# One decoder step, first stage and attention: a PE order table, one transpose and the sample tables moved

## The chip, the core and the metric

The kernel runs on one core of one Trainium2 chip, in fp32. Its time is the device time of one execution in microseconds. The engines are named as the profile names them: PE (TensorE), ACT (ScalarE), DVE (VectorE), POOL (GpSimd), SP (SyncE).

## What is computed

One inference step of a one-layer decoder, for 512 prompt tokens and for 8 sequences of 8 sample tokens with 2048 cached tokens each. Forgetting attention (FoX) and sparse attention (NSA) run side by side on the same normed input:

```python
def layer_sample(x, c, fox_pool, logf_pool, nsa_pool, win_buf, page_table, lp):
    pm = pre_mixer(x, c, lp)          # h = rms_norm(x) * (1 + scale(c)) + shift(c); z = h @ w_in; split
    o_fox = fox_attend(...)           # over all cached keys, with forget gates
    nsa_all = jnp.concatenate([gather_pages(nsa_pool, page_table), pm['nsa_rows']], axis=1)
    kc, vc, c_end = compressed_kv(nsa_all[:, :, 0], nsa_all[:, :, 1], lp)
    o_nsa = nsa_attend(...)           # compressed, selected and window keys, three gates
    y = post_mixer(x, pm, o_fox, o_nsa, lp)   # branches, gates, output projection, MLP

def compress_blocks(x, pos, w1, w2):
    xc = x[:, :n_chunk * CMP_STRIDE].reshape(b, n_chunk, CMP_STRIDE, NSA_GROUPS, HEAD_DIM)
    lead = jnp.einsum('bncgd,cdh->bngh', xc + pos[0], w1[0])
    trail = jnp.einsum('bncgd,cdh->bngh', xc + pos[1], w1[1])
    return jnp.einsum('bngh,hd->bngd', jax.nn.silu(lead[:, :-1] + trail[:, 1:]), w2)
```

`compressed_kv` applies `compress_blocks` to the raw keys and values and norms the keys' result. The prompt's layer is the same without a cache.

## The kernel before

`Step.first_stage` (L549) compresses the cached keys and values. It works in 48 units: four pieces (j) by keys and values (kv) for batches 0, 1, 2 and 3 alone (units 0 to 31), then for batches 4 and 5 together (32 to 39) and 6 and 7 together (40 to 47). In a unit u:

- `cmp_order` (L458, asked two units ahead) copies a piece of the pages `cpg` into a tile `ro` on DVE (three buffers),
- `rows_turn` (L467), for unit u + 1, transposes `ro` on PE ("ct"), ACT copies the result to `x`, and the sum of its halves goes to `xs`: on DVE for one batch, on POOL (L485) for two,
- `cmp_hidden` (L487), for unit u, multiplies `x` and `xs` with the weights ("hid", "hids"),
- then the functions of `todo[u]` run, a table written out by hand (L614 to 664).

PE's order is the order of the calls: `link` (L93) chains each matmul and transpose behind the one before. The other engines' orders come from a scheduler that sees the dependences. From `todo` come, among others:

- for each of five x tiles `norm` (ACT square, DVE inverse root in small steps), `scaled` (ACT) and `turned` (eight PE transposes "nt", two ACT copies "adw<-nt"); the tuple (n, v, u) gives the three units, (28, 30, 31) and (29, 31, 33) for the last two,
- the eight parts of the modulation, `ada_first` ("ada" on PE, "adap" on ACT) and one unit later `ada_end` ("adat" on PE, a sum on DVE); `modulate` (L816) applies a pair of them to the turned tiles,
- `cmp_act` and `cmp_silu` (the activation of a group of units, "cst" and "csx"), `cmp_out` (products "co", keys then normed into "knn") at units 18/19, 34/35, 42/43, and `cmp_keys` (L542: two transposes "kct" of knn, one ACT copy) at units 21, 37, 45.

In this stage the PSUM tag "mm" has two banks, in turn for ada, nt's first half, nt's second half, adat, co and kct. A tile there waits until the reader of the tile two before has finished.

`prompt_attention` (L1083) runs in steps: four heads each of the selected ("slc"), window ("win") and FoX branches. A step asks the scores of its own head (`scores`, group 0), then the values of the head before last (`weigh`, L1343), then its scores of group 1, and the transposes of the head before (`turn_over`, `factors`). For a "slc" head, `cmp_turn` (L1388) transposes the compressed weights "cm" (four PE transposes "ct<-identF,cm" and a copy to the upper part of cm), called right behind `factors` (L1157); `weigh` uses the result in the "oc" products behind the sixteen "oslc" products.

`sample_tables` (L1554) is asked at step n = 9, so that it runs among the FoX heads. It makes masks and ramps for the sample attention: large ones on POOL (`gp`), 29 small ones on DVE (`self.ts`, `self.tt`, `self.cp`). POOL also makes the copies "ffox<-denfox" (`scale`, L1308) that PE's "fcfox" transposes (`factors`) read.

Of the kernel before, what the change touches and what calls it, by code (L numbers as in the profile page):

```python
# [11 lines left out]
OP = mybir.AluOpType  # L12
# [34 lines left out]
class Step:  # L47
# [501 lines left out]
    def first_stage(self, pl, pe, hf, seam):  # L549
# [69 lines left out]
        for k, (n, v, u) in enumerate(((18, 21, 23), (20, 23, 25), (22, 25, 27), (28, 30, 31), (29, 31, 33))):  # L619
            todo[n] += [lambda k=k: norm(k)]  # L620
            todo[v] += [lambda k=k: scaled(k)]
            todo[u] += [lambda k=k: turned(k)]
# [23 lines left out]
        for k, u in enumerate((26, 30, 32, 34, 36, 38, 40, 42)):  # L646
            todo[u] += [lambda k=k: ends.update({k: self.ada_first(pe, ada[k])})]
            todo[u + 1] += [lambda k=k: ends[k]()]
            if k > 1:
                todo[(27, 31, 33, 35, 37, 39)[k - 2]] += [wada(k)]  # L650
            if k % 2:
                todo[max(u + 2, 35)] += [lambda k=k: self.modulate(0, hf, range(k - 1, k + 1))]
# [8 lines left out]
        for i in range(3):  # L661
            for kv in range(2):
                todo[(18, 34, 42)[i] + 1 - kv] += [lambda i=i, kv=kv: self.cmp_out(pl, i, kv)]
            todo[(21, 37, 45)[i]] += [lambda i=i: self.cmp_keys(i)]
# [418 lines left out]
    def prompt_attention(self, pk, pn, pp):  # L1083
# [22 lines left out]
        for n, (br, r) in enumerate(steps + [(None, None)] * 2):  # L1106
# [49 lines left out]
            if prev:  # L1156
                held = pbr, pr, T, pf, self.cmp_turn(pr, pw) if pbr == "slc" else None  # L1157
# [185 lines left out]
    def weigh(self, pn, br, r, T, F, cT):  # L1343

        u = f"{br}{r}"
        out = self.oT[:, r + (0 if br == "fox" else 4), 0:SEQ]
# [207 lines left out]
    def sample_tables(self):  # L1554
# [19 lines left out]
        self.ts(hot, ei, self.prow, None, OP.is_equal)  # L1574
# [10 lines left out]
        for g in range(2):  # L1585
            nbf = self.carve([NS, NB, 8])
            self.tt(nbf, self.nbf[:, g], tmask[:NS], OP.add)
            own = self.nbA[g].rearrange("p (i x) -> p i x", x=80)
            for o in range(2):
                self.cp(own[32 * o:32 * o + 32, :, 8 * o:8 * o + 8], nbf[32 * o:32 * o + 32, o::2])  # L1590
        own = self.nbW.rearrange("p (i x) -> p i x", x=80)
        for o in range(2):
            self.cp(own[64 * o:64 * o + 64, :, 8 * o:8 * o + 8], tramp[64 * o:64 * o + 64, 0:4])
# [12 lines left out]
        self.ts(pos, self.h_row, 4.0, -4.0, OP.is_ge, OP.mult)  # L1606
        self.tt(pos, pos, self.h_row, OP.add)
        self.ts(lim, pos, 0.0, 4.0, OP.is_equal, OP.mult)
        self.tt(lim, lim, pos, OP.add)
        self.ts(self.tok, ej, lim, None, OP.is_lt)  # L1610
        self.ts(self.hot.rearrange("p (h t) -> p h t", t=8), ej[:, :, None].to_broadcast([P, 8, 8]), self.t_row, None, OP.is_equal)

        self.ts(pos, self.g_row, 15.0, 1.0, OP.mult, OP.add)
        self.ts(lim, self.prow, 64.0, slope, OP.is_ge, OP.mult)
        for g in range(2):
            self.ts(low[:, g:g + 1], lim, pos, 0.0625 ** g, OP.mult, OP.mult)
        step, new = self.carve([P, 4]), self.carve([P, 2, 8])
        self.iota(step, [[512, 4]], base=-2048)
        for g in range(2):
            self.ts(self.base[:, :, g], step, low[:, g:g + 1], None, OP.mult)  # L1620
            self.iota(new[:, g], [[1, 8]], base=512)
            self.ts(new[:, g], new[:, g], low[:, g:g + 1], None, OP.mult)
            self.tt(new[:, g], new[:, g], tmask[:, 0], OP.add)
            own = self.nbA[g].rearrange("p (i x) -> p i x", x=80)
            for o in range(2):
                v = slice(64 + 32 * o, 96 + 32 * o)
                self.cp(own[v, :, 8 * o:8 * o + 8], new[v, g, None, :].to_broadcast([32, 4, 8]))
# [1109 lines left out]
```

## Time and profile before

| | |
|---|---|
| median of 3 runs | 1149.58 us (1149.41, 1149.58, 1157.79) |
| profiled execution | 1149.83 us, span 1148.2 us |
| mean granted PE clock | 0.997 |
| HBM | 217.64 MB read, 57.12 MB written |

The profile has one execution. Times in it are microseconds from the span's start. A row of a timeline gives the start, the length, engine, line of kernel.py, operation and tiles (out<-in), a count where rows were joined, and in brackets the idle time of the engine ahead of the row with what ended it. Matmuls are pipelined, so that a row's length overlaps the next row. In a table of groups the numbers behind the bar are busy microseconds, mean nanoseconds of one, and idle time ahead. The first stage takes about the first 165 us of the span, prompt attention lies between about 290 and 430.

### The profile page before, as it was taken

What the parts mean: (1) busy time and instruction counts of PE and PEld (TensorE: products, weight loads), DVE (VectorE), ACT (ScalarE), POOL (GpSimd) and SP (SyncE); (2) the same over time, 40 slices, a digit from 0 to 9 for tenths busy, and PEclk for the clock granted to TensorE, in tenths of its full rate; (3) what the DMA queues carried; (4) which work ended last, traced back from release to release, by engine and by line L of the source; (5) the groups of instructions that cost most, each with busy time, mean ns of one, the idle gap of its engine ahead of it and who ended that gap; (6) DMA issues with size and microseconds to landing.
All of it is one profiled execution on the core that took longest, in us unless ns stands there. A gap on an engine that the chain in (4) does not pass through costs nothing.

```text
span 1148.2 us, 25279 instructions
## 1 busy us (share of the span) xinstructions
PE 1120.8 (98%) x9530; PEld 971.6 (85%) x9530; DVE 768.8 (67%) x1841; ACT 576.6 (50%) x1101; POOL 306.5 (27%) x366
## 2 busy tenths in 40 slices
PE   8989999999999999999999999999999999999998
PEld 5987889999676666777899999789999998888887
DVE  3655576686788875666654446668776754798686
ACT  1455453354777775555432324356565655565420
POOL 5313320000321150001666573001655511110000
PEclk9999999999999999999999999999999999999999
DMA  9998445796586587999889986356444537977732
GB/s 237 250 265 227 144 125 195 242 335 210 194 273 201 185 287 251 295 314 337 226 260 290 327 274 221 103 161 211 135 150 154 184 113 254 319 261 255 249 105 83
DMA packets 188188, 255.52 MB, mean 223 GB/s; under 512 B 23161, under 2 KB 144706, under 8 KB 185890
## 3 DMA queue, kind: packets, MB, share of 16 engines
q1 hardware_dynamic: 148770, 173.03, 48.5%
q0 software_dynamic: 21296, 67.38, 17.8%
q10 hardware_dynamic: 18000, 13.50, 3.9%
q8 instruction: 75, 1.23, 0.4%
q14 instruction: 47, 0.39, 0.1%
HBM read 217.64 MB, written 57.12 MB: 239 GB/s over the span
## 4 chain that ended last, share of the span: by engine, by line
PE 82%; DVE 8%; DMA 4%; issue 3%; ACT 2%; SPq 1%; POOL 1%; POOLq 0%; ACTq 0%; DVEq 0%
PE dn L83 14%; PE mg L83 9%; PE z L83 8%; PE br L83 4%; PE wo L83 3%; PE hid L83 3%; PE up L83 3%; PE k L89 3%; DMA cpg<-in_cache_nsa_kv 2%; PE ss L83 2%; PE so L83 2%; PE dns L83 2%; PE ct L89 2%; PE ada L83 1%; PE hids L83 1%
## 5 line engine op out<-in xcount | busy, mean ns | idle before, releaser
L83 PE MATMUL z<-winh,h 128*128 128x264 f32 (+1 forms) x576 | 110.5, 286 | 0.1
L83 PEld LDWEIGHTS z<-winh,h 128*128 128x128 f32 x576 | 91.6, 190 | 1.6 <-issue 0.8
L83 PE MATMUL z<-winl,h 128*128 128x264 f32 (+1 forms) x320 | 88.1, 284 | 0.2 <-DVE winl L137 0.2
L83 PE MATMUL mg<-hH,wmh 128*128 128x288 f32 x240 | 70.5, 295 | 0.0
L83 PE MATMUL mg<-hH,wml 128*128 128x288 f32 x240 | 70.2, 294 | 0.0
L83 PE MATMUL mg<-hL,wmh 128*128 128x288 f32 x240 | 68.5, 296 | 0.0
L83 PE MATMUL hid<-x,w1raw 128*128 128x128 f32 (+1 forms) x384 | 66.8, 318 | 0.2 <-ACT x L118 0.2
L83 PEld LDWEIGHTS z<-winl,h 128*128 128x128 f32 x320 | 60.6, 190 | 0.4 <-DVE winl L137 0.4
L83 PEld LDWEIGHTS hid<-x,w1raw 128*128 128x128 f32 x384 | 56.1, 197 | 3.4 <-ACT x L118 0.5
L118 ACT ACTIVATE x<-ct 128x512 f32<-128x512 f32 x64 | 36.4, 594 | 42.9 <-PE ct L89 28.5
L137 DVE TENSOR_TENSOR wml<-wmr,wmh 128x1024 fp32r<-128x1024 f32 x14 | 22.5, 1604 | 42.7 <-ACT wmh L118 42.7
L83 PEld LDWEIGHTS mg<-hH,wmh 128*128 128x128 f32 x240 | 45.1, 188 | 0.1
L83 PEld LDWEIGHTS mg<-hH,wml 128*128 128x128 f32 x240 | 45.0, 188 | 0.0
L83 PEld LDWEIGHTS mg<-hL,wmh 128*128 128x128 f32 x240 | 44.3, 188 | 0.0
L137 DVE TENSOR_TENSOR wp<-sums,wp 128x1024 fp32r<-128x1024 f32 x26 | 36.8, 1424 | 10.5 <-ACT wp L118 10.0
L137 DVE TENSOR_TENSOR wp<-pu,wp 128x512 fp32r<-128x512 f32 (+1 forms) x26 | 31.7, 1224 | 17.6 <-ACT wp L118 17.6
L118 ACT ACTIVATE mgt<-mg 128x288 f32<-128x288 f32 x32 | 12.6, 407 | 52.7 <-PE mg L83 52.6
L118 ACT ACTIVATE u<-u 128x1152 f32<-128x1152 f32 x29 | 33.6, 1159 | 10.8 <-DVE u L106 10.0
L2097 POOL TENSOR_TENSOR td<-td,td 128x512 f32<-128x512 f32 x24 | 33.2, 1384 | 21.2 <-DMA td<-in_w_down 20.5
L2097 POOL TENSOR_TENSOR td<-td 128x512 f32<-128x512 f32 x24 | 33.9, 1414 | 15.8 <-DMA td<-in_w_down 15.6
L89 PE MATMUL ct<-identF,ro 128*128 128x128 f32 x256 | 36.6, 277 | 1.5 <-DVE ro L121 1.5
L83 PE MATMUL br<-oL,wbh 128*128 128x288 f32 x128 | 37.8, 295 | 0.0
(1176 smaller groups left out, 3581.5 us busy)
## 6 DMA issues: line engine op xcount, KB each, us to landing
adw<-in_w_ada SPq DMA_DIRECT2D x16, 1024.0 KB
foxD<-in_cache_fox_kv SPq DMA_DIRECT2D x128, 128.0 KB
rows<-in_cache_nsa_kv SPq DMA_DIRECT2D x128, 128.0 KB
rows<-foxD SPq DMA_DIRECT2D x26, 512.0 KB
pu<-in_w_up SPq DMA_DIRECT2D x26, 512.0 KB
wdr<-in_w_down SPq DMA_DIRECT2D x26, 512.0 KB
cpg<-in_cache_nsa_kv SPq DMA_DIRECT2D x96, 128.0 KB
td<-in_w_down POOLq DMA_DIRECT2D x24, 512.0 KB, 6.3
```

Of the source, the lines that this page charges most:

```text
L83: ins = self.nc.tensor.matmul(out, a, b, start=start, stop=stop, skip_group_check=True)
L89: ins = self.nc.tensor.transpose(out, in_, self.identF[:n, :n])
L118: return self.nc.scalar.activation(out, in_, f, **kw)
L137: self.splits.append((eng or self.nc.vector).tensor_tensor(l, x, h.bitcast(F32), op=OP.subtract).ins)
L2097: self.nc.gpsimd.tensor_tensor(out, x, y, op=OP.subtract)
```

## The change

Four things move; nothing is added or left out.

1. In `first_stage` the keys' transposes go from units (21, 37, 45) to (24, 39, 46).
2. There too the last two x tiles go from (28, 30, 31) and (29, 31, 33) to (30, 32, 33) and (33, 36, 37), and `modulate` for the first two pairs of parts to unit 38 and 39 at the earliest.
3. `cmp_turn` is called at the head of `weigh`, one step later, and no longer behind `factors`.
4. The 29 small instructions of `sample_tables` go to POOL.

```diff
--- before.py
+++ after.py
@@ -616,7 +616,7 @@
         todo[10] += [self.ada_turned, lambda: self.cmp_bias(pe, 0), lambda: self.cmp_bias(pe, 1)]
         todo[12] += [self.cmp_bias_end]
 
-        for k, (n, v, u) in enumerate(((18, 21, 23), (20, 23, 25), (22, 25, 27), (28, 30, 31), (29, 31, 33))):
+        for k, (n, v, u) in enumerate(((18, 21, 23), (20, 23, 25), (22, 25, 27), (30, 32, 33), (33, 36, 37))):
             todo[n] += [lambda k=k: norm(k)]
             todo[v] += [lambda k=k: scaled(k)]
             todo[u] += [lambda k=k: turned(k)]
@@ -649,7 +649,7 @@
             if k > 1:
                 todo[(27, 31, 33, 35, 37, 39)[k - 2]] += [wada(k)]
             if k % 2:
-                todo[max(u + 2, 35)] += [lambda k=k: self.modulate(0, hf, range(k - 1, k + 1))]
+                todo[max(u + 2, 37 + (k + 1) // 2)] += [lambda k=k: self.modulate(0, hf, range(k - 1, k + 1))]
         self.lfg = {}
         for y, u in enumerate((32, 35)):
             todo[u] += [pinned(lambda y=y: self.stage_logf(pe, y))]
@@ -661,7 +661,7 @@
         for i in range(3):
             for kv in range(2):
                 todo[(18, 34, 42)[i] + 1 - kv] += [lambda i=i, kv=kv: self.cmp_out(pl, i, kv)]
-            todo[(21, 37, 45)[i]] += [lambda i=i: self.cmp_keys(i)]
+            todo[(24, 39, 46)[i]] += [lambda i=i: self.cmp_keys(i)]
         self.cmp_warm(50)
         self.cmp_order(pl, 0)
         self.cmp_taps(0)
@@ -1154,7 +1154,7 @@
             if prev:
                 pf = self.factors(pn, f"{pbr}{pr}", pF)
             if prev:
-                held = pbr, pr, T, pf, self.cmp_turn(pr, pw) if pbr == "slc" else None
+                held = pbr, pr, T, pf, pw
             prev = None
             if br is None:
                 continue
@@ -1340,9 +1340,11 @@
         self.act(F, tb)
         return F
 
-    def weigh(self, pn, br, r, T, F, cT):
+    def weigh(self, pn, br, r, T, F, cw):
 
         u = f"{br}{r}"
+        if br == "slc":
+            cT = self.cmp_turn(r, cw)
         out = self.oT[:, r + (0 if br == "fox" else 4), 0:SEQ]
         ob = self.accb(f"o{u}")
         cv = {"slc": C_SV, "win": C_WV, "fox": C_FV}[br]
@@ -1571,7 +1573,7 @@
         ei, hot = self.carve([P, 32]), self.carve([P, 32])
         self.iota(ei, [[1, 32]])
-        self.ts(hot, ei, self.prow, None, OP.is_equal)
+        gp.tensor_scalar(hot, ei, self.prow, None, op0=OP.is_equal)
...
         for g in range(2):
             nbf = self.carve([NS, NB, 8])
-            self.tt(nbf, self.nbf[:, g], tmask[:NS], OP.add)
+            gp.tensor_tensor(nbf, self.nbf[:, g], tmask[:NS], op=OP.add)
             own = self.nbA[g].rearrange("p (i x) -> p i x", x=80)
             for o in range(2):
-                self.cp(own[32 * o:32 * o + 32, :, 8 * o:8 * o + 8], nbf[32 * o:32 * o + 32, o::2])
+                gp.tensor_copy(own[32 * o:32 * o + 32, :, 8 * o:8 * o + 8], nbf[32 * o:32 * o + 32, o::2])
...
-        self.ts(pos, self.h_row, 4.0, -4.0, OP.is_ge, OP.mult)
-        self.tt(pos, pos, self.h_row, OP.add)
...
+        gp.tensor_scalar(pos, self.h_row, 4.0, -4.0, op0=OP.is_ge, op1=OP.mult)
+        gp.tensor_tensor(pos, pos, self.h_row, op=OP.add)
...
```

PE in the first stage, units 20 to 24, before (hids and hid are the products of a unit, ct the turn of the next, kct the keys' transposes):

```order
L83 MATMUL hids_883<-xs_116,w1sum 128x128 x2
L89 MATMUL kct_1100<-identF,knn_973 128x128 x2
L89 MATMUL ct_1106<-identF,ro_3_996 128x128 x4
L83 MATMUL hid_881<-x_113,w1raw 128x128 x4
L83 MATMUL hids_883<-xs_114,w1sum 128x128 x2
```

and with the change:

```order
L83 MATMUL hids_883<-xs_116,w1sum 128x128 x2
L89 MATMUL ct_1102<-identF,ro_3_996 128x128 x4
L83 MATMUL hid_881<-x_113,w1raw 128x128 x4
L83 MATMUL hids_883<-xs_114,w1sum 128x128 x2
L89 MATMUL ct_1142<-identF,ro_0_1100 128x128 x4
L83 MATMUL hid_882<-x_115,w1raw 128x128 x4
L83 MATMUL hids_883<-xs_116,w1sum 128x128 x2
L89 MATMUL nt_00_1155<-identF,x_857 128x128 x4
L89 MATMUL nt_01_1161<-identF,x_857 128x128 x4
L89 MATMUL ct_1170<-identF,ro_0_1100 128x128 x4
L83 MATMUL hid_881<-x_113,w1raw 128x128 x4
L83 MATMUL hids_883<-xs_114,w1sum 128x128 x2
L89 MATMUL kct_1185<-identF,knn_973 128x128 x2
```

The kct transposes now stand behind three more units and the first x tile's nt.

ACT in the first stage around the copies of x tile 3's transposes (adw<-nt_30 and nt_31; nss is the sum of squares of a tile, nrs its inverse root), before:

```order
L118 ACTIVATE x_1187<-x_1187,nrs_3_1294 128x1024
L118 ACTIVATE cst_1474<-hid_882,cmpb 128x256
L118 ACTIVATE cst_1427<-csx_1426 128x512
L118 ACTIVATE x_1266<-x_1266,nrs_4_1379 64x1024
L118 ACTIVATE adw<-nt_30_1452 128x4x128
L118 ACTIVATE adw<-nt_31_1458 128x4x128
```

and with the change:

```order
L118 ACTIVATE cst_1439<-csx_1438 128x512
L118 ACTIVATE x_1183<-x_1183,nrs_3_1375 128x1024
L118 ACTIVATE adap_1478<-ada_1479 128x256
L118 ACTIVATE x_113<-ct_1493 128x4x128
L118 ACTIVATE x_113<-ct_1499 128x4x128
L118 ACTIVATE sq_1524,nss_4_1525<-x_1266 64x1024
L118 ACTIVATE adw<-nt_30_1512 128x4x128
L118 ACTIVATE adw<-nt_31_1518 128x4x128
```

The scaling of the last tile (x_1266, nrs_4) has left the place ahead of the adw copies, and its square (sq, nss_4) stands there.

POOL among the FoX heads, between the second and the third copy ffox, before (scr and fscr hold the tables):

```order
L1315 COPY ffox_5766<-denfox_5687 128x512
L1598 TENSOR_SCALAR scr<-scr,slope_i 128x512
L736 TENSOR_TENSOR fscr<-fscr,Dt 128x256
L1584 TENSOR_TENSOR scr<-scr 128x64
L1599 TENSOR_TENSOR scr<-scr 128x512
L738 TENSOR_TENSOR fscr<-fscr 128x8x8
L131 IOTA scr 128x512 x2
L739 TENSOR_TENSOR fscr<-fscr 128x8x8
L1630 TENSOR_SCALAR scr<-scr 128x512
L1315 COPY ffox_6025<-denfox_5948 128x512
```

and with the change:

```order
L1315 COPY ffox_5766<-denfox_5687 128x512
L1600 TENSOR_SCALAR scr<-scr,slope_i 128x512
L1610 TENSOR_SCALAR scr<-scr 128x1
L736 TENSOR_TENSOR fscr<-fscr,Dt 128x256
L1586 TENSOR_TENSOR scr<-scr 128x64
L1589 TENSOR_TENSOR scr<-nbf,scr 64x64 x2
L1601 TENSOR_TENSOR scr<-scr 128x512
L1611 TENSOR_TENSOR scr<-scr 128x1
L738 TENSOR_TENSOR fscr<-fscr 128x8x8
L1595 COPY scr<-scr 64x4x8 x2
L1592 COPY scr<-scr 32x4x8 x4
L1315 COPY ffox_6025<-denfox_5948 128x512
```

Ten of the moved instructions stand between the two copies now; the large IOTA and the first L1630 of before went behind the later one.

More of the change, by code (lines that the diff above doesn't have):

```diff
@@ L1586, in sample_tables @@
             nbf = self.carve([NS, NB, 8])
-            self.tt(nbf, self.nbf[:, g], tmask[:NS], OP.add)
+            gp.tensor_tensor(nbf, self.nbf[:, g], tmask[:NS], op=OP.add)
             own = self.nbA[g].rearrange("p (i x) -> p i x", x=80)
             for o in range(2):
-                self.cp(own[32 * o:32 * o + 32, :, 8 * o:8 * o + 8], nbf[32 * o:32 * o + 32, o::2])
+                gp.tensor_copy(own[32 * o:32 * o + 32, :, 8 * o:8 * o + 8], nbf[32 * o:32 * o + 32, o::2])
         own = self.nbW.rearrange("p (i x) -> p i x", x=80)
         for o in range(2):
-            self.cp(own[64 * o:64 * o + 64, :, 8 * o:8 * o + 8], tramp[64 * o:64 * o + 64, 0:4])
+            gp.tensor_copy(own[64 * o:64 * o + 64, :, 8 * o:8 * o + 8], tramp[64 * o:64 * o + 64, 0:4])
         rw = self.rw
@@ L1605, in sample_tables @@
         self.iota(ej, [[1, 8]])
-        self.ts(pos, self.h_row, 4.0, -4.0, OP.is_ge, OP.mult)
-        self.tt(pos, pos, self.h_row, OP.add)
[L1608 to L1614, printed above, removed]
+        gp.tensor_scalar(pos, self.h_row, 4.0, -4.0, op0=OP.is_ge, op1=OP.mult)
+        gp.tensor_tensor(pos, pos, self.h_row, op=OP.add)
+        gp.tensor_scalar(lim, pos, 0.0, 4.0, op0=OP.is_equal, op1=OP.mult)
+        gp.tensor_tensor(lim, lim, pos, op=OP.add)
+        gp.tensor_scalar(self.tok, ej, lim, None, op0=OP.is_lt)
+        gp.tensor_scalar(self.hot.rearrange("p (h t) -> p h t", t=8), ej[:, :, None].to_broadcast([P, 8, 8]), self.t_row, None, op0=OP.is_equal)
+        gp.tensor_scalar(pos, self.g_row, 15.0, 1.0, op0=OP.mult, op1=OP.add)
+        gp.tensor_scalar(lim, self.prow, 64.0, slope, op0=OP.is_ge, op1=OP.mult)
         for g in range(2):
-            self.ts(low[:, g:g + 1], lim, pos, 0.0625 ** g, OP.mult, OP.mult)
+            gp.tensor_scalar(low[:, g:g + 1], lim, pos, 0.0625 ** g, op0=OP.mult, op1=OP.mult)
         step, new = self.carve([P, 4]), self.carve([P, 2, 8])
@@ L1619, in sample_tables @@
         for g in range(2):
-            self.ts(self.base[:, :, g], step, low[:, g:g + 1], None, OP.mult)
+            gp.tensor_scalar(self.base[:, :, g], step, low[:, g:g + 1], None, op0=OP.mult)
             self.iota(new[:, g], [[1, 8]], base=512)
-            self.ts(new[:, g], new[:, g], low[:, g:g + 1], None, OP.mult)
-            self.tt(new[:, g], new[:, g], tmask[:, 0], OP.add)
+            gp.tensor_scalar(new[:, g], new[:, g], low[:, g:g + 1], None, op0=OP.mult)
+            gp.tensor_tensor(new[:, g], new[:, g], tmask[:, 0], op=OP.add)
             own = self.nbA[g].rearrange("p (i x) -> p i x", x=80)
@@ L1626, in sample_tables @@
                 v = slice(64 + 32 * o, 96 + 32 * o)
-                self.cp(own[v, :, 8 * o:8 * o + 8], new[v, g, None, :].to_broadcast([32, 4, 8]))
+                gp.tensor_copy(own[v, :, 8 * o:8 * o + 8], new[v, g, None, :].to_broadcast([32, 4, 8]))
         for g in range(2):
```

## The prediction

> **What bounds the kernel now.** I read the page's busy shares first, then the waits of TensorE (PE).
>
> ```profile
> PE 1120.8 (98%) x9530; PEld 971.6 (85%) x9530; DVE 768.8 (67%) x1841; ACT 576.6 (50%) x1101; POOL 306.5 (27%) x366
> PE kct L89 <- DVE knn L106: 2.6, 1, 2.6
> PE adat L89 <- ACT adw L118: 2.6, 3, 2.1
> ```
>
> PE is busy 98% of the span. The change removes no matmul, so it can win only PE's idle time and what the clock loses with it. In the waits the columns are microseconds in total, times, longest: two single waits of over 2 us stand out, both in the first stage. PE's timeline shows them in place, idle time in brackets.
>
> ```profile
> 62.11 0.61 PE L83 MATMUL hids<-xs,w1sum 128*128 128x128 f32 x4
> 65.36 0.69 PE L89 MATMUL kct<-identF,knn 128*128 128x128 f32 x2 [2.64 <-DVE knn L106]
> 91.59 1.09 PE L89 MATMUL nt<-identF,x 128*128 128x128 f32 x8 [0.43 <-ACT x L118]
> 94.78 0.44 PE L89 MATMUL adat<-identF,adap 128*128 128x128 f32 x2 [2.10 <-ACT adw L118]
> 95.93 3.58 PE L83 MATMUL hid<-x,w1raw 128*128 128x256 f32 x8
> ```
>
> The hid product behind the second wait takes 3.58 us (the same shape at 102.23, below: 1.89). So I cut the trace into windows of 3.41 us, counted from 65.20, where the clock falls. Columns: length, busy PE, PEld, DVE, ACT, POOL, then the granted clock.
>
> ```profile
> 0.35:3.76 3.41, 1.51 (x4) 0.57 (x5) 2.31 (x27) 1.49 (x2) 2.72 (x9) 1.00 0.48 139
> 61.79:65.20 3.41, 0.93 (x9) 0.74 (x7) 3.00 (x15) 0.80 (x3) 0.00 (x0) 1.00 1.04 289
> 65.20:68.61 3.41, 3.25 (x15) 3.25 (x16) 1.98 (x11) 2.14 (x5) 0.00 (x0) 0.50 1.04 315
> 92.51:95.92 3.41, 1.31 (x12) 1.14 (x11) 2.54 (x9) 3.28 (x6) 0.00 (x0) 1.00 1.06 300
> 95.92:99.33 3.41, 3.41 (x10) 2.70 (x9) 1.74 (x3) 2.35 (x4) 0.98 (x1) 0.50 1.01 236
> 444.08:447.49 3.41, 2.34 (x19) 1.86 (x18) 2.66 (x9) 2.68 (x7) 0.00 (x0) 1.00 0.95 315
> ```
>
> A window with 0.93 or 1.31 us of PE work is followed by one at half clock. The window with 1.51 us at the start is not, nor is the one at 444.08, all of whose PE work is transposes. So each long wait costs twice: kct 2.64 + half of the 3.25 us that PE worked at clock 0.50 = **4.26 us**; the x tile 0.43 + 2.10 + half of 3.41 = **4.23 us**.
>
> **The change part by part.**
>
> *Keys.* The kct transposes move behind three more units on PE; their instructions stay the same. Is knn ready then?
>
> ```profile
> 64.88 0.42 DVE L106 TENSOR_TENSOR knn<-co,knr 128x256 f32<-128x256 f32 x1
> 68.96 0.60 PE L89 MATMUL ct<-identF,ro 128*128 128x128 f32 x4
> 70.73 1.04 PE L89 MATMUL nt<-identF,x 128*128 128x128 f32 x8
> ```
>
> knn ends at 65.30, and in the new DVE order three small instructions more stand ahead of it. A unit takes 1.77 us (68.96 to 70.73). From the last sums' end, 62.72, PE reaches kct after 3 units and one nt group (about 0.9): 62.7 + 5.3 + 0.9 = 68.9. The margin is over 2 us: the wait goes, with its slow window. 4.26 saved; if the pages feeding DVE's ro copies were late instead, nothing of it (rival below). The other two kct, two units and one unit later, have no wait in the list: 0.
>
> *Last two x tiles.* Their squares, scaling and transposes move one to four units later; the wait of 0.43 for x goes if the scaling is in time. The 2.10 was not for x: adat follows nt in the two PSUM banks and takes the bank of nt's first half, so it waits for ACT's adw copy. This stays so at unit 33, where the ACT queue now has, ahead of that copy: a tanh, the scaling of x tile 3, adap, two x copies and the last tile's square.
>
> ```profile
> 88.72 1.09 PE L89 MATMUL ct<-identF,ro 128*128 128x128 f32 x8
> 100.30 1.07 PE L83 MATMUL ada<-wada,adw 128*32 128x256 f32 x16
> 102.23 1.89 PE L83 MATMUL hid<-x,w1raw 128*128 128x256 f32 x8
> 104.92 0.70 PE L89 MATMUL nt<-identF,x 64*128 64x64 f32 x8
> 85.20 1.04 ACT L118 ACTIVATE sq<-x 64x1024 bf16<-64x1024 f32 x1
> 88.86 0.39 ACT L118 ACTIVATE adap<-ada 128x256 f32<-128x256 f32 x1 [1.00 <-PE ada L83]
> 89.42 1.08 ACT L118 ACTIVATE x<-ct 128x512 f32<-128x512 f32 x2 [0.17 <-PE ct L89]
> 90.39 1.15 ACT L118 ACTIVATE x<-x,nrs 128x1024 f32<-128x1024 f32 x1
> 95.11 0.62 ACT L118 ACTIVATE cst<-csx 128x512 f32<-128x512 f32 x1
> 90.58 0.15 DVE L106 TENSOR_TENSOR ntt<-nrs 64x1 f32<-64x1 f32 x1
> 90.65 1.27 POOL L485 TENSOR_TENSOR xs<-x 128x512 f32<-128x512 f32 x1 [0.61 <-DVE nrs L115]
> 90.76 1.17 DVE L106 TENSOR_TENSOR ntt<-ntt,nth 64x1 f32<-64x1 f32 x1
> ```
>
> PE's side: the first two-batch ct comes 4.26 earlier, at 84.5. From it to the next unit's ct are 2.4 (ct 0.9, narrow hid 0.9, sums 0.5, with gaps) and 0.3 for adat. Then come two wide units, the second with an ada product ahead of it: 100.30 to 104.92 = 4.6 with the ada, 3.6 without its 1.0. So nt starts at 84.5 + 2.4 + 0.3 + 3.6 + 4.6 = 95.4 and ends at 96.3.
> ACT's side: the tanh came 6.4 us behind the ct before (88.72 to 95.11); now 84.5 + 6.4 + 1.3 for the two ro copies that DVE has ahead of it = 92.2. Behind it ACT needs 0.6 + 1.1 + 0.4 + 1.0 + 1.2 = 4.3, the adw copy 0.6 more: 97.1, a wait of 0.8. That holds one POOL sum in DVE's way, as there was. The last three rows show it: a DVE instruction that starts while POOL adds xs ends when POOL does, 1.17 long where its neighbour of the same shape takes 0.15. A second sum, that of the next unit, may fall into DVE's chain: 1.1 more, and were nt to wait for x as well, up to 3.0 in all. With no sum in the way nothing is left to wait for but the copy itself, 0.2. Between 0.2 and 3.0 I take 1.5, near the middle: one sum surely, the second in part. One wait of 1.5 leaves 1.9 of 3.41 busy, over the 1.51 that kept the clock, so no slow window. Saved: 4.23 − 1.5 = **2.7**, from −0.5 (3.0 and a slow window of 1.7) to 4.0.
>
> *Modulate* and the adap that goes with it move up to three units later, to ACT and DVE with idle time there (busy 2.35 and 1.74 of 3.41 at 95.92): 0.
>
> *Compressed weights.* Four PE transposes and one ACT copy per head move from behind the factors to the head of the values, past the next scores.
>
> ```profile
> 310.66 0.63 PE L89 MATMUL ct<-identF,cm 128*64 128x128 f32 x4 [0.84 <-DVE cm L106]
> 312.52 2.37 PE L83 MATMUL oslc<-PTslc,zN 128*64 128x512 f32 x16
> L118 ACT ACTIVATE cm<-ct x4: 577/590/595, 311.3 to 370.2; 64x512 f32<-64x512 f32 x4
> ```
>
> Only the first of four heads waits: 0.84. In the new place eight swin products lie ahead (what PE does here between ct and 312.52, 1.5 us), more than the wait. The ACT copy, 0.59, must end before the oc products behind oslc, 2.3 us later: covered. Without that cover each head would lose about 0.6. I take **0.8**, range 0 to 0.8.
>
> *Tables.* 29 small instructions leave DVE for POOL, among the FoX heads.
>
> ```profile
> 410.24 0.98 PE L89 MATMUL ptfox<-identF,Sfox 128*128 128x128 f32 x7 [0.43 <-DVE nbf L121]
> 414.27 0.63 PE L89 MATMUL fcfox<-identF,ffox 128*128 128x128 f32 x4 [1.37 <-DVE nmfox L1302]
> 410.22 1.95 DVE L121 COPY scr<-scr 32x32 f32<-32x32 f32 x4
> 416.00 1.08 POOL L131 IOTA scr<- 128x512 f32 x2 [4.24 <-DVE scr L121]
> 418.86 0.60 POOL L1315 COPY ffox<-denfox 128x512 f32<-128x512 f32 x1
> 426.62 0.63 POOL L1315 COPY ffox<-denfox 128x512 f32<-128x512 f32 x1 [5.32 <-DVE denfox L1310]
> L131 POOL IOTA scr<- 128x8 f32 x3 | 0.4, 139 | 0.0
> L1583 POOL TENSOR_SCALAR scr<-scr,t_row 128x64 f32<-128x64 f32 x1 | 0.6, 570 | 0.1
> ```
>
> PE's two waits, 0.43 + 1.37 = 1.8, are for DVE instructions (score sums among them) that stand behind table work, 1.95 us of it in one row. With the tables gone they come sooner. On POOL one instruction is bounded by 0.14 (IOTA 128x8) and 0.57 (TENSOR_SCALAR 128x64): 4 to 16.5 us for 29, where POOL idled 4.24 + 5.32 close by. Queued behind them are the ffox copies, for which fcfox waits: 14 of the 29 stand ahead of the third, 2 to 8 us; 4.24 of idle time plus some 5 between that copy (418.86) and its fcfox, ten us behind the one at 414.27, hold that. POOL will at times stop DVE, as above. I take **1.5**, from −1.0 to 2.1.
>
> By the Trainium skill, Advanced Engine Details and Errata, section VectorE Performance Modes, GpSimd shares the Vector engine's second SBUF port and the two block each other, which speaks against this move. The row at 90.76 agrees (1.17 us instead of 0.15); if every moved instruction blocked DVE so, DVE would gain nothing from losing them, the tables would bring 0 and the sum would be 7.8.
>
> Sum: 4.3 + 2.7 + 0.8 + 1.5 = 9.3 us. The profiled execution took 1149.8, against a median of 1149.6 (1149.4 and 1157.8 beside it), so 1149.8 (a span of 1148.2 and 1.6 around it) − 9.3 = **1140.5 us**.
>
> **The rivals.**
>
> *All waits go.* With both sums clear of DVE's chain and the tables at their best: 4.3 + 4.2 + 0.8 + 2.1 + 0.4 for small waits = 11.8, 1138.0. For it: ACT has little to do there. Against: adat still stands behind nt in a two-bank ring. Chance 0.14.
>
> *The x tile's wait moves to unit 33 whole.* 3.0 idle, the window falls to half clock: the term is −0.5, so 4.3 − 0.5 + 0.8 + 1.5 = 6.1, 1143.7. For it: the square stands in ACT's queue ahead of the adw copy, and POOL sums held DVE. Against: the window must fall so that it holds less than 1.5 us of work. Chance 0.21.
>
> *Pages are late.* PE runs 4.3 earlier into DVE's ro copies and waits for the page there; then 2.7 + 0.8 + 1.5 = 5.0, 1144.8. In the trace DVE waits once for a page before 110, 0.3 us, which speaks against. Chance 0.05.
>
> *The slow windows stay.* The half clock at 65.20 and 95.92 has another cause than the waits before it. Then 1.6 + 1.7 stay lost: 9.3 − 3.3 = 6.0, 1143.8. Against: both follow the two emptiest windows of the stage, and no other window of it is slow. Chance 0.02. By the Trainium skill, TensorE: Matmul & The Clock Gate, section Why this matters for your kernels, PE gaps up to about 3 us don't drop the clock, which would speak for this rival; the trace differs, with 0.50 behind gaps of 2.64 and 2.10.
>
> *POOL is too slow; slower than before.* The 29 have fixed costs of their own and take as long as the 1.27 us row (90.65) each. Ahead of the third ffox copy stand then 18 us against some 7.5 of slack: fcfox waits 10, and the tables lose 11 instead of winning 1.5. 4.3 + 2.7 + 0.8 − 11 = −3.2: 1153.0. It turns the total from about 1.1 us per instruction on. Against: rows of 0.14 to 0.57 for such shapes. Chance 0.04.
>
> **How the numbers follow.** The forecast has 0.54: 1138.9 to 1142.3, from the x term's 4.0 and 1.2 (waits of 0.2 and 3.0, no slow window) and 0.3 for the smaller terms. The range takes in the first rival's 1138.0 and the second's and third's ends: 1137.6 to 1145.4. A measurement of this kernel tells about 1% from no change, here 11.5 us: faster means under 1138.1. Only the first rival reaches that, in most of its cases: 0.12. Slower than 1161 needs the last rival at over twice its price or something unseen: 0.03. Same: 0.85.
>
> **What would show it.** Right: no wait of kct on knn, no clock below 1.00 between 60 and 105; adat at about 92 to 97 waiting 0.5 to 2.5 on ACT adw at full clock; no wait of ct on cm; fcfox and ptfox together under 0.6. Wrong: a half-clock window near 97 to 102 (second rival), ct waiting on ro or its pages (third), POOL ahead of ffox with fcfox waiting on it (fourth), or waits on hidden products' x copies, which I take as in time.

## The result and the profile after

The kernel before: 1152.21 us, median of 15 executions (1148.99 to 1157.79). The changed kernel: 1143.46 us, median of 15 (1140.26 to 1150.79). The ratio is 0.9933, with a 95% interval of 0.9914 to 0.9952: some 8 us less, within 1%, so "same" by the bound that the prediction set. The 1143.46 lies in the range (1137.6 to 1145.4), not in the forecast's own (1138.9 to 1142.3). The profiled execution took 1140.26, a span of 1138.6; against the profiled one of before that is −9.6, where the sum said −9.3. Most of the document is on why the terms behind these two near equal numbers are not equal, and where the other 2 to 3 us of the median are.

The page's busy shares and PE's waits of the changed kernel (total, times, longest):

```profile
PE 1114.6 (98%) x9530; PEld 968.2 (85%) x9530; DVE 763.3 (67%) x1812; ACT 576.9 (51%) x1101; POOL 316.0 (28%) x395
PE ct L89 <- DVE ro L121: 3.2, 2, 1.9
PE z L83 <- ACT kcT L118: 0.9, 1, 0.9
PE swin L83 <- DVE nmwin L1302: 0.6, 1, 0.6
```

The 29 instructions show on DVE (1841 to 1812) and POOL (366 to 395). The 2.6 of kct is gone, adat's longest went from 2.1 to 1.3 (below), and two waits are new: z for kcT, swin for nmwin. PE in the first stage and at its end:

```profile
67.31 1.04 PE L89 MATMUL nt<-identF,x 128*128 128x128 f32 x8
69.95 0.27 PE L89 MATMUL kct<-identF,knn 128*128 128x128 f32 x1
98.42 0.44 PE L89 MATMUL adat<-identF,adap 128*128 128x128 f32 x2 [1.29 <-ACT adw L118]
99.56 1.89 PE L83 MATMUL hid<-x,w1raw 128*128 128x256 f32 x8
159.28 0.51 PE L83 MATMUL z<-winh,h 128*128 128x264 f32 x2 [0.93 <-ACT kcT L118]
```

kct stands without a wait at 69.95 (predicted 68.9; PE ran 0.9 behind before's execution at 32 us, and then 3.4 ahead). The nt of the first x tile, at 70.73 before, is at 67.31. adat comes at 98.42 and waits 1.29 (predicted at 92 to 97, 0.5 to 2.5), and the hid product behind it takes 1.89, the full clock, where before's took 3.58. The next two rows are the windows that the wait falls on, in the columns of the prediction. They are counted in steps of 3.413 us from 5.58, where PE's clock rises in this execution (the products at the kernel's start come every 0.43 us ahead of it and every 0.22 behind it):

```profile
94.33:97.74 3.41, 2.79 (x17) 2.27 (x16) 0.69 (x1) 3.41 (x7) 1.63 (x2) 1.00 1.00 264
97.74:101.15 3.41, 2.73 (x18) 2.56 (x19) 2.96 (x18) 3.41 (x9) 0.53 (x1) 1.00 1.02 316
```

Here the adat wait is shared between two windows, which keep 2.79 and 2.73 us of work (1.9 in one was predicted), and the clock stays, as the 1.89 of the hid product shows. In three of the experiments below the same 1.29 falls into one window whole and leaves 2.11 to 2.13; the clock stays there too. What made the wait is ACT's queue and DVE's chain ahead of it (ACT's rows first, then DVE's and POOL's):

```profile
93.95 0.63 ACT L118 ACTIVATE cst<-csx 128x512 f32<-128x512 f32 x1 [2.99 <-issue]
96.74 1.05 ACT L118 ACTIVATE sq<-x 64x1024 bf16<-64x1024 f32 x1
97.78 1.06 ACT L118 ACTIVATE adw<-nt 128x512 f32<-128x512 f32 x2
87.28 0.16 DVE L115 SCALAR_TENSOR_TENSOR nrs<-ntt,nti 128x1 f32<-128x1 f32 x1
87.47 1.26 DVE L106 TENSOR_TENSOR ntt<-nrs 128x1 f32<-128x1 f32 x1
91.47 1.25 DVE L106 TENSOR_TENSOR modT<-adas,chT 128x18 f32<-128x18 f32 x1
87.44 1.27 POOL L485 TENSOR_TENSOR xs<-x 128x512 f32<-128x512 f32 x1 [0.61 <-DVE nrs L115]
91.04 1.64 POOL L485 TENSOR_TENSOR xs<-x 128x512 f32<-128x512 f32 x1 [2.32 <-ACT x L118]
```

Both POOL sums held DVE: 1.26 and 1.25 for instructions that work on 1 and 18 elements per partition. The tanh (cst<-csx) starts at 93.95, not at 92.2, and the square has ACT from 96.74 until the adw copies.

In the attention `link` chains only a part of PE's instructions, and the scheduler places the rest. The rows below are of before, then of the changed kernel, and show the products ofox of the second FoX head (the kernel asks for eight, and the trace has two records of each, sixteen in all). A group with a count begins when its first one does:

```profile
417.23 1.07 PE L83 MATMUL ofox<-PTfox,zF 128*64 128x512 f32 x2
418.23 0.55 PE L89 MATMUL ptfox<-identF,Sfox 128*128 128x128 f32 x3
418.71 1.07 PE L83 MATMUL ofox<-PTfox,zF 128*64 128x512 f32 x4
419.71 0.55 PE L89 MATMUL ptfox<-identF,Sfox 128*128 128x128 f32 x3
420.19 1.58 PE L83 MATMUL ofox<-PTfox,zF 128*64 128x384 f32 x10
```

```profile
305.95 0.50 PE L83 MATMUL swin<-khwin,qstnsa 128*128 128x512 f32 x1 [0.57 <-DVE nmwin L1302]
306.52 0.60 PE L89 MATMUL ct<-identF,cm 128*64 128x128 f32 x4
410.34 2.38 PE L83 MATMUL ofox<-PTfox,zF 128*64 128x512 f32 x16
```

ct on cm waits no more; a scores product ahead of it now does, 0.57. And ofox, whose sixteen products stood in three pieces with transposes between (1.07 + 1.07 + 1.58), runs in one piece of 2.38. The prediction had none of that.

The same PE instruction's start in both traces, after less before, tells where the time went:

| place | after − before, us | step | predicted |
|---|---|---|---|
| first pages, at 32 us | +0.9 | two waits for ro are longer (3.2 against 1.5) | 0 |
| behind the first kct | −3.4 | keys −4.3 | −4.3 |
| unit 37 | −6.6 | last x tiles −3.3 (no slow window, a shorter wait) | −2.7 |
| first z behind the stage | −5.4 | last kct +1.0, small differences | 0 |
| values of the selected heads | −5.4 | −0.3, taken between neighbouring rows | −0.8 |
| end of FoX | −9.1 | tables −3.6 | −1.5 |
| end | −9.6 | −0.5 in small pieces | 0 |

The first row is of the execution, not of the change: the same two waits take 3.8, 3.1 and 3.1 in the profiles of the values, the tables and the pairs below, whose first stage is that of before.

### The profile page after: what moved, and what is told of

It reads as the page before. It is cut to its first block, busy times and chain, and to the rows that moved or that the text cites. A ratio compares the mean times of both kernels' runs of the same rounds, so it can differ in the third digit from the quotient of the medians.

```text
span 1138.6 us, 25281 instructions
## 1 busy us (share of the span) xinstructions
PE 1114.6 (98%) x9530; PEld 968.2 (85%) x9530; DVE 763.3 (67%) x1812; ACT 576.9 (51%) x1101; POOL 316.0 (28%) x395
## 4 chain that ended last, share of the span: by engine, by line
PE 82%; DVE 7%; DMA 6%; SPq 2%; ACT 2%; issue 2%; ACTq 0%; DVEq 0%
PE dn L83 14%; PE mg L83 9%; PE z L83 6%; PE br L83 4%; PE wo L83 4%; PE up L83 3%; DMA cpg<-in_cache_nsa_kv 3%; PE hid L83 3%; PE k L89 3%; PE ss L83 2%; DMA winr<-in_w_in 2%; PE so L83 2%; PE dns L83 2%; SPq L168 2%; PE ct L89 2%
## 5 line engine op out<-in xcount | busy, mean ns | idle before, releaser
L83 PE MATMUL hid<-x,w1raw 128*128 128x128 f32 (+1 forms) x384 | 64.2, 310 | 0.2 <-ACT x L118 0.2
```

Of the source, the lines that this page charges most:

```text
L83: ins = self.nc.tensor.matmul(out, a, b, start=start, stop=stop, skip_group_check=True)
```

## Experiments: the four parts alone

Theory: the sum above holds part by part. Rival for each part: its wait only changes its name. Each part was put alone into the kernel before; the runs of this group share 31 executions of before, median 1152.14 (1148.83 to 1159.66).

**Keys alone.** Edit:

```diff
-            todo[(21, 37, 45)[i]] += [lambda i=i: self.cmp_keys(i)]
+            todo[(24, 39, 46)[i]] += [lambda i=i: self.cmp_keys(i)]
```

> The kernel before with only the keys' transposes at units 24, 39, 46. My theory: the wait of 2.64 us for knn goes and the half-clock window behind it with it, 4.3 us by 72 us of the span; the last kct, one unit later, makes the first z product wait about 1 us at the seam; the x tile's wait (2.5 us and, by the place of its window, 1.7 more or not) stays. Net 2.5 to 4 us, a ratio of 0.997. Rival, pages late: the wait returns as ct on ro between 62 and 70 and nothing is gained. Rival, slow windows have another cause: the clock falls near 65 all the same and 2.6 is gained there.

Measured: 1153.28 (1145.25 to 1155.36, 10 executions), ratio 0.9984 [0.9956, 1.0012]. In the profile kct has no wait and PE gains 4.1 us between 49 and 79 against before's trace. But the execution as a whole gained nothing (span 1153.7): two other windows fell to the half clock. One was an early one, behind a wait of 2.2 for ro that before's profile had at 1.1:

```profile
30.10:33.51 3.41, 1.19 (x10) 1.02 (x11) 1.39 (x6) 0.05 (x1) 1.72 (x4) 1.00 1.09 240
33.51:36.92 3.41, 3.41 (x19) 3.41 (x18) 1.02 (x2) 0.78 (x2) 1.58 (x3) 0.50 1.07 237
```

So the step is right where it was made, and its 4.3 do not come out in the time: 2.5 to 4 were expected, and the means of the executions differ by 1.2. The interval allows 0 to 5 us less, or up to 1.4 more.

**Last x tiles alone** (with `modulate`). Edit:

```diff
-... (28, 30, 31), (29, 31, 33))):
+... (30, 32, 33), (33, 36, 37))):
-                todo[max(u + 2, 35)] += ...
+                todo[max(u + 2, 37 + (k + 1) // 2)] += ...
```

> The kernel before with only the last two x tiles and modulate moved. My theory: the knn wait stays at 2.6 us; the wait of 0.43 of nt on x goes, adat behind nt half a unit later waits 1.3 us on ACT's adw copy instead of 2.1, without a half-clock window: 1.2 to 3.3 us gained, a ratio of 0.998. Rival: the wait comes back whole at unit 33 with a half-clock window and nothing is gained.

Measured: 1149.85 (1146.87 to 1152.97), ratio 0.9974 [0.9954, 0.9995], some 3 us. adat waits 1.29 here too, with no half clock behind it. The surprise is at kct, which was left in its old place and waits its 2.64 as before:

```profile
61.37:64.78 3.41, 1.83 (x15) 1.41 (x12) 2.66 (x15) 2.04 (x5) 1.28 (x3) 1.00 1.07 310
64.78:68.20 3.42, 2.02 (x18) 2.02 (x19) 3.16 (x15) 1.54 (x3) 0.00 (x0) 1.00 1.03 308
98.91:102.33 3.42, 2.13 (x19) 1.87 (x18) 1.65 (x13) 3.42 (x7) 1.25 (x1) 1.00 1.00 317
```

The same wait falls on the border of two windows, which keep 1.83 and 2.02 of work, and the clock stays. The last row is the window of adat. A new wait, hids for POOL's xs, 0.69 at 119.29, is taken up below.

**Values alone.** Edit:

```diff
-                held = pbr, pr, T, pf, self.cmp_turn(pr, pw) if pbr == "slc" else None
+                held = pbr, pr, T, pf, pw
-    def weigh(self, pn, br, r, T, F, cT):
+    def weigh(self, pn, br, r, T, F, cw):
+        if br == "slc":
+            cT = self.cmp_turn(r, cw)
```

> The kernel before with only the compressed weights' transposes at the head of the values. By the prediction 0.8 us are gained, as the wait of ct on cm goes. Rival, from the changed kernel's trace: the scores that now come first wait 0.57 us on DVE's nmwin, so that 0.2 to 0.3 us are left. Either is too small for the median: the waits decide.

Measured: 1152.87 (1146.15 to 1158.35), ratio 0.9987 [0.9956, 1.0017]: nothing that the time can tell. Locally:

```profile
314.72 0.50 PE L83 MATMUL swin<-khwin,qstnsa 128*128 128x512 f32 x1 [0.54 <-DVE nmwin L1302]
```

cm's 0.84 is gone, 0.54 of it is back as a wait for a row maximum that DVE owes the first swin. 0.3 stay.

**Tables alone.** Edit: the 29 instructions of `sample_tables`, as in part 4 of the change:

```diff
-        self.ts(hot, ei, self.prow, None, OP.is_equal)
+        gp.tensor_scalar(hot, ei, self.prow, None, op0=OP.is_equal)
...
```

> The kernel before with only the tables on POOL. By the prediction's step 1.5 to 1.9 us are gained, the waits of ptfox on nbf (0.43) and of fcfox on nmfox (1.37). My theory now: 3.6 us, since the order of PE also changes there: the ofox products of one head, which stood in runs of 2, 4 and 10 with transposes between them (3.5 us), stand together as 16 (2.4 us). Rival: POOL holds DVE and gives part of it back, under 1.5 us. Medians: a ratio of 0.997.

Measured: 1147.78 (1143.31 to 1149.05), ratio 0.9953 [0.9928, 0.9979], 2.4 to 8.3 us. This is the largest part in the time (the means differ by 5.2), and in the profile 3.7 us between 384 and 450. Both waits (nbf, nmfox) are gone, and the second head's sixteen ofox run in one piece, as in the changed kernel. Three windows of its first stage:

```profile
65.06:68.47 3.41, 1.61 (x15) 1.62 (x16) 3.15 (x14) 1.14 (x3) 0.00 (x0) 1.00 1.05 316
92.37:95.78 3.41, 1.32 (x13) 1.08 (x12) 2.54 (x11) 3.19 (x6) 0.00 (x0) 1.00 1.05 316
95.78:99.19 3.41, 3.41 (x11) 2.78 (x10) 1.82 (x3) 2.44 (x4) 0.89 (x1) 0.50 1.00 229
```

These are waits that this kernel kept: kct's 2.64 leaves 1.61 in its window, and the clock stays; adat's leaves 1.32, and it falls.

## Experiments: the disputed costs by themselves

The next four share 19 executions of before, median 1151.3 (1147.97 to 1155.93).

**Is the clock half of a wait's price really bought by idle time in one window?** Before, with the adat wait (2.10) filled: nine products of the identity go ahead of the first adat.

```diff
+        if ch == 0:
+            fill = self.trb("fill")
+            for _ in range(9):
+                self.mm(fill, self.identB, self.identB[:, None, :].to_broadcast([P, 4, P]), True, True)
         tb = self.sideb(f"adat{ch}")
```

> The kernel before with nine products of the identity (128x512, into a bank that the next ct overwrites) on PE between nt of x tile 3 and the adat that waits 2.10 us: PE's order is else the same, the wait is filled with 1.9 us of work of no use. In four profiles of kernels with this wait a half-clock window stood behind it, four of four. My theory: a window is slow because PE did under about 1.35 us of work in the one before; filled, the clock stays at 1.00 there and 1.7 us are gained though PE does more. Rival, slow windows have another cause: the clock falls near 96 all the same, the time is the same or longer. Median: a ratio of 0.9985 or 1.000.

```profile
93.96 2.10 PE L83 MATMUL fill<-identB 128*128 128x512 bf16 x9
97.37 1.89 PE L83 MATMUL hid<-x,w1raw 128*128 128x256 f32 x8
94.30:97.71 3.41, 3.26 (x21) 2.05 (x19) 2.37 (x7) 3.41 (x7) 0.00 (x0) 1.00 1.06 298
```

2.10 of useless work takes the place of 2.10 of waiting, and the hid behind it takes 1.89 instead of 3.58. By itself this does not settle the question. Without the fill this window would have held about 1.5 us (3.26 less the 1.76 of fill in it), and in the profile of the pairs, the next run, the same wait stands unfilled (2.09), falls otherwise on the windows, and the clock stays, with hid at 1.89 as well:

```profile
92.13:95.54 3.41, 1.74 (x14) 1.31 (x13) 3.34 (x11) 2.74 (x4) 1.28 (x1) 1.00 0.98 323
```

What speaks against a cause apart from idle time is all traces together. The first 165 us of the fourteen profiles of this document have 658 windows, counted from where the clock first rises in each. Ten hold up to 1.36 us of PE work, and all ten are followed by half clock; ten hold 1.44 to 1.87, and two are; of the others that ran at full clock one is, with 2.01. So a nearly empty window is followed by a slow one, whatever emptied it, and between 1.4 and 2.0 these traces do not say which way it goes.

The time shows no gain: 1152.48 (1149.34 to 1159.79), ratio 1.0011 [0.9987, 1.0036]. The granted clock times the span says what an execution lost to the clock: 3.5 us in the mean here, 2.1 in the executions of before beside it.

**Why did the tables give more than their waits?** Theory: in before DVE's late answers made the scheduler put transposes between the pairs of ofox products, and split pairs cost. Edit in before, tables left on DVE: the first ofox product is chained behind the last transpose of the next head.

```diff
                 o += P
+        self.last_turn = self.last_tr
...
+                if br == "fox" and k + g == 0:
+                    self.behind(self.last_mm, self.last_turn.name)
```

> The kernel before with one more order on PE: a FoX head's ofox products start behind the last transposes of that head's weights. The tables stay on DVE. It moves six transposes of the second head and ten of the fourth from between the ofox products to ahead of them. My theory: the products of one head run 1.2 us faster together (2.4 us for 16 instead of 1.0 + 1.0 + 1.5), so about 1.2 us are gained at the second head and up to 0.6 at the fourth, with the waits for nbf and nmfox as before. Rival: the split products only filled the time until DVE and ACT had copied the weights; together they wait as long for the copies and nothing is gained. Median: a ratio of 0.9985 or 1.000.

Measured: 1150.56 (1149.12 to 1152.58), ratio 0.9989 [0.9972, 1.0006].

```profile
414.03 0.63 PE L89 MATMUL fcfox<-identF,ffox 128*128 128x128 f32 x4 [1.37 <-DVE nmfox L1302]
417.65 2.60 PE L83 MATMUL ofox<-PTfox,zF 128*64 128x512 f32 x16
```

The wait for nmfox stays at 1.37, and yet PE gains 1.25 us at the second head and 0.65 at the fourth against before's trace, with no product less: the ofox products of all four heads keep PE busy for 11.2 us instead of 13.0. So about 1.25 of the tables' 3.6 came by order, not by a wait. The interval is too wide for the 1.9 to show in the time.

**Can the 1.29 of adat be had?** Edit in the changed kernel: the last tile's square one unit later.

```diff
-... (33, 36, 37))):
+... (34, 36, 37))):
```

> The changed kernel with the last x tile's square one unit later, so that it stands behind ACT's adw copies of tile 3 and not ahead of them. My theory: ACT's queue sets the wait of adat; without the square's 1.2 us the copy starts when nt's first half is written, and the wait of 1.29 us falls to about 0.2, 1.1 us gained. Rival: DVE, held by the POOL sums, is late for more than ACT, and 0.8 or more of the wait stays.

One execution: 1146.81. adat's wait falls from 1.29 to 0.28, as the theory of the square in ACT's queue has it. But three us of it, and more, are lost again 20 us later (PE; then POOL; then windows):

```profile
97.52 0.44 PE L89 MATMUL adat<-identF,adap 128*128 128x128 f32 x2 [0.28 <-ACT adw L118]
118.41 1.43 PE L83 MATMUL hids<-xs,w1sum 128*128 128x256 f32 x4 [3.19 <-POOL xs L485]
116.04 1.02 POOL L713 DMA_INDIRECT lfg<-in_cache_fox_logf,lfrow  x1 [9.54 <-DMA lfD<-lfg]
115.70:119.11 3.41, 0.70 (x3) 0.65 (x4) 0.00 (x0) 0.00 (x0) 3.06 (x3) 1.00 0.26 77
```

The window with 0.70 of work is followed by two at half clock; with the wait about 6.6 us are lost. The second gather of the forget logarithms (lfg, issued by POOL) waits 9.54 us for a store (lfD, issued by SP) that reads the one buffer the gather writes; the sum xs stands behind it in POOL's queue, and PE's hids behind that. Does the changed kernel have this too?

**The seam.** Edit in the changed kernel: the third kct one unit earlier.

```diff
-            todo[(24, 39, 46)[i]] += [lambda i=i: self.cmp_keys(i)]
+            todo[(24, 39, 45)[i]] += [lambda i=i: self.cmp_keys(i)]
```

> The changed kernel with the last kct back at unit 45. My theory: the wait of 0.93 us of the first z product on ACT's kcT goes, since kct's bank is read one unit earlier, and kct itself does not wait for knn (no such wait stood before the change): 0.9 us gained. Rival: the wait comes from the seam whatever the kct's unit, and z waits as long for something else.

One execution: 1144.69. z's wait of 0.93 for kcT is gone, worth 0.7 to 0.9 there, so unit 46 is the cause of that wait: z takes the bank that the third kct's copy on ACT frees late. This execution too had the POOL wait, 2.93 at 118.58, and two slow windows.

## Experiments: the gather

The last four are kernels made from the changed one, side by side, with 13 executions of before (median 1152.83). Theory: the changed kernel, being 7 us ahead at unit 38 while SP's store is not, loses time to the gather in part of its executions. Rival: what differs between executions is the clock alone.

The changed kernel again, as the yardstick:

> The changed kernel once more, as the standard for the next three on the same chip: a ratio of 0.993 to the kernel before, executions between 1140 and 1151 us. My theory for the spread: in part of the executions the second gather of log forget values on POOL waits so long for the store of the first that the sum queued behind it on POOL makes PE wait (3 us and up to two half-clock windows), at about 115 us.

and with a second buffer, so that the gather need not wait for the store:

```diff
-t = pe.tile([P, 512], F32, tag="lfg", bufs=1, name=f"lfg{y}")
+t = pe.tile([P, 512], F32, tag="lfg", bufs=2, name=f"lfg{y}")
```

> The changed kernel with a second buffer for the gathered log forget values, so that POOL's second gather does not wait for the store of the first; each engine's order is the same. My theory: the wait of PE's hids for POOL's xs at 115 to 119 us (0.7 to 3.2 in three of the four profiles of kernels with the moved x tiles) never comes; the mean of the executions falls by 1 to 3 us against the changed kernel on the same chip, the slowest ones most. Rival: the spread has other causes (pages, the clock) and the mean stays within 0.5 us.

The changed kernel: 1141.28 to 1147.97 in seven executions (an eighth took 2198.61 and is left out of the mean and the ratio), mean 1144.0, ratio to before 0.9926 [0.9902, 0.9951]. With two buffers: 1140.66 (1139.33 to 1142.41, six), mean 1140.6, ratio 0.9891 [0.9865, 0.9916]. The difference of the means is 3.3 (1 to 3 were expected), with an interval, worked out from the two spreads, of about 1.0 to 5.6. The gather on POOL: before, the changed kernel's first profile, its second, and with two buffers:

```profile
114.98 1.03 POOL L713 DMA_INDIRECT lfg<-in_cache_fox_logf,lfrow  x1 [0.16 <-issue]
```

```profile
112.63 1.02 POOL L713 DMA_INDIRECT lfg<-in_cache_fox_logf,lfrow  x1 [5.23 <-DMA lfD<-lfg]
```

```profile
PE hids L83 <- POOL xs L485: 1.6, 1, 1.6
115.45 1.02 POOL L713 DMA_INDIRECT lfg<-in_cache_fox_logf,lfrow  x1 [7.91 <-ACT x L118]
116.63:120.05 3.42, 2.01 (x14) 1.49 (x15) 0.26 (x2) 0.66 (x2) 3.28 (x3) 1.00 0.51 114
120.05:123.46 3.41, 3.41 (x14) 3.10 (x13) 3.13 (x13) 1.20 (x2) 0.60 (x1) 0.50 0.90 314
```

```profile
107.28 1.02 POOL L713 DMA_INDIRECT lfg<-in_cache_fox_logf,lfrow  x1 [0.16 <-issue]
```

Before, POOL reaches the gather at 114.8 and the store has landed. Changed, POOL reaches it at 107.4 and stands until 112.6, which PE did not notice, or until 115.4, which cost PE 1.6 and a window at half clock. The store itself does not come earlier: SP issues it at 103.9 in before's profile and at 104.6 and 110.5 in these two. (The releaser named in that row, ACT x, had long been done; the wait is the store's, as its absence with a second buffer shows.) The theory holds. About 1.6 of the 3.3 is the clock that follows the wait: the changed kernel's executions lost 2.0 us to it in the mean, those with two buffers 0.4.

The two others. Sums: the xs sums of two batches on DVE instead of POOL, to test what held DVE:

```diff
-self.splits.append(self.nc.gpsimd.tensor_tensor(xs, x[:, 0:2], x[:, 2:4], op=OP.add).ins)
+self.splits.append(self.nc.vector.tensor_tensor(xs, x[:, 0:2], x[:, 2:4], op=OP.add).ins)
```

> The changed kernel with the two-batch sums xs on DVE and not on POOL. My theory: POOL's sums hold DVE (instructions of 0.16 take 1.25 beside them); on DVE a sum takes about 0.7 and holds nothing, so the tanh of unit 33 comes 1 us earlier and adat waits 0.3 to 0.6 us instead of 1.29; PE has no wait for POOL's xs near 118. Rival: the square alone sets that wait, which stays at 1.3.

One execution: 1139.96. adat's wait falls to 0.25; and PE does not wait for the gather, though it comes as late as ever, since no sum stands behind it:

```profile
97.99 0.44 PE L89 MATMUL adat<-identF,adap 128*128 128x128 f32 x2 [0.25 <-ACT adw L118]
89.25 0.14 DVE L106 TENSOR_TENSOR ntt<-nrs 128x1 f32<-128x1 f32 x1
90.98 0.17 DVE L106 TENSOR_TENSOR modT<-adas,chT 128x18 f32<-128x18 f32 x1
115.03 1.29 POOL L713 DMA_INDIRECT lfg<-in_cache_fox_logf,lfrow  x1 [10.92 <-DMA lfD<-lfg]
```

The two DVE instructions that took 1.26 and 1.25 beside POOL's sums take 0.14 and 0.17 here, so it was the sums that held them.

All: two buffers, the square at 34, the third kct at 45 and the chained ofox pairs, each as in its diff above.

> The changed kernel with four edits: the second buffer for the gather, the last tile's square one unit later, the last kct at unit 45, and a FoX head's ofox products behind the last transposes of its weights. By the single runs: 1 to 3 for the gather, 1.0 for the square, 0.9 for the seam, 0.6 for the fourth FoX head's products. Against the changed kernel 3 to 5 us faster, a ratio of 0.989 to 0.991 to the kernel before. Rival: each stall only moves to the next (as the wait of nt and adat did), under 1.5 us are left.

Measured: 1140.65 (1138.64 to 1143.79, six), ratio 0.9895 [0.9868, 0.9921], the same as with two buffers alone, though all three local gains are in its profile (span 1137.3). This misses what was expected of the three beyond the gather: what they give is under what six executions tell, and the clock stood against them (1.9 us lost in the mean, 0.4 with two buffers alone; in the profile an early window at half clock behind the ro wait). With two buffers the kernel is 0.989 of before, the best of those run more than once, and one line more than the change.

## Why the prediction was right, and where it was not

**Keys: the mechanism right, 4.3 in the profile; the price half by luck.** The 2.64 of waiting is gone in every profile with the keys moved. The 1.62 of clock was there in the profiled execution of before, but it was not a property of the wait. Six profiles have a kct that waits those 2.64. A half-clock window follows in two, where the wait left 0.93 (before) and 1.36 (pairs); it does not in four, where the emptiest window of the wait held 1.44 (values), 1.61 (tables), 1.83 (x tiles) and 2.05 (fill). Within one execution the windows lie on a fixed grid: 65.20 and 95.92 of before are nine times 3.41 apart. From one execution to the next the grid lies elsewhere, so that one wait costs once or twice. By the Trainium skill, TensorE: Matmul & The Clock Gate, section What's actually happening, the window of 3413 ns is free-running and its place differs from run to run; these traces agree, with a first rise of the clock anywhere from 5.33 to 7.41 us. The step that failed is "each long wait costs twice", a reading of one execution taken as an expectation. Executions of before lost 2.9 us to the clock in the mean (3.2, 2.1 and 3.3 in the three groups, 63 executions), those of the changed kernel 2.1 (22). So about 0.8 us of clock was saved in the mean, less than the groups of before differ, and not the 3.3 of the two slow windows. The profiled execution lost none and is the fastest of its 15; but another of them that lost none took 1143.93, so the clock is not all that sets them apart.

**"The 1.51 that kept the clock" was misread.** The row at 0.35 does not show it. PE was at half speed from its first product to 7.17 us, the window behind that row included; the clock column says 1.00 there because the record of the clock only begins at 7.17. The same product, ahead of and behind that point (count, busy us, mean ns of one):

```profile
L83 PE MATMUL idle<-identB 128*128 128x512 bf16 x8 | 3.6, 631 | 0.0
L83 PE MATMUL idle<-identB 128*128 128x512 bf16 x32 | 7.1, 379 | 0.0
```

So the prediction had no row for where the clock stays between 1.31 and 2.34. That 1.9 of work is enough was right, as the windows of 2.11 to 2.13 show, but one with 2.01, 0.7 of it transposes of 64x64, was followed by half clock (in the fences on the gather). What besides busy time decides stays open. Another reading fails without changing a term: before 110 DVE waits for a page not once but twice, 0.34 and, at 30.42, 1.81.

**Last x tiles: right.** A wait of 1.29 where 1.5 was taken, at full clock. It came at 98.42, behind the 92 to 97 of the signs. But both POOL sums fell into DVE's chain, where one and part of the second were counted, and nt did not wait for x. The square's unit and the sums' engine each free the wait (0.28, 0.25), so both are needed for it.

**The third kct: 0 predicted, about 0.9 lost.** "The other two have no wait in the list: 0" looked at the wait the edit removes, not at the one it makes: who takes kct's PSUM bank next. The z products do.

**Compressed weights: 0.3 instead of 0.8.** The transposes' own cover was right; the wait went on to the next instruction that DVE was late for, the scores product. The prediction's step "eight swin products lie ahead, more than the wait" took them as ready.

**Tables: 3.6 instead of 1.5**, over the upper end of 2.1. The waits gave their 1.8 whole, so what POOL held of DVE cost PE nothing that shows; two waits of ptfox for PTfox, 0.7 together, stay as before, so that the sign "fcfox and ptfox together under 0.6" holds for nbf and nmfox alone. Of the rest 1.25 is order, shown by the chained pairs; for the last 0.5 no run here has a cause. Products that fill different halves of 64 columns overlap when they stand side by side (in the changed kernel their records start 0.01 us apart); a transpose between the two of a pair parts them. By the Trainium skill, TensorE: Matmul & The Clock Gate, section Part 3: Packing small matmuls — row/col tiling, products in different column groups of the array run at once, three of 32 columns 2.38 times as fast as one after another; the traces agree as far as they show it, sixteen in 2.38 us together, and in 1.00 + 1.00 + 1.58 = 3.6 when parted twice (417.23 to 418.23, 418.71 to 419.71, and the last row). The result of 0 for this part did not come: single DVE rows are held by POOL (1.26 against 0.16 at 87), the path was not. The rule that the prediction names beside it, of the Trainium skill, Advanced Engine Details and Errata, section VectorE Performance Modes, speaks only of Vector instructions in a two-port mode, which the section does not list for tensor_tensor; the held rows are of that operation.

**What no rival had: a queue that does not get faster.** The rivals asked whether PE would wait for pages, POOL tables or ACT; POOL's queue in the first stage was seen only as the place of sums. PE and POOL run 7 us ahead, the store on SP does not, and 3.3 us of mean are lost behind the gather. These and the three errors of size nearly cancel: 4.3 + 3.3 − 1.0 + 0.3 + 3.6 − 0.9 = 9.6 in the profile (two small pieces of 0.5 cancel beside them), some 8 in the medians. That 9.6 stands so near the 9.3 is luck in part: the −0.9 is of the execution, and the 3.3 of clock in the first two terms is more than an average execution wins. That the median lies near the second rival's 1143.7 says nothing for it: its half-clock window behind adat is not there.

## What to carry to other kernels

A wait's price in clock is a chance, not a sum: count the waiting itself as won, and the slow window only by the share of executions in which the grid lets it fall. When an engine runs ahead by an edit, ask of each in-order queue that it drains what stands there for something that did not move, here a gather behind a store, with work behind it that the fast engine needs. And when an edit empties a queue, look at how the order of another engine changes, since it may be worth as much as the wait.

## What was not expected of the hardware

- The same wait of 2.64 us was followed by half clock in two profiles and not in four, by how it fell on windows of 3.41 us. Windows with up to 1.36 us of PE work were followed by half clock ten times of ten, ones with 1.44 to 1.87 twice of ten, once one with 2.01; behind one with 0.70 and one with 1.09 two windows were slow.
- The same sixteen products of 64 columns take 2.4 us in one piece and 3.6 in three.
- A sum of 128x512 on POOL held a DVE instruction on one element per partition for 1.26 us; with the sum on DVE it took 0.14.
